# Summing the last layer's modulation on ScalarE, GpSimd and VectorE beside the second FFN, in place of TensorE beside the even mixer

## The chip, the cores and the metric

One core of a Trainium2 chip runs the whole program in one launch. The metric is the device time in microseconds (us). TensorE is called PE here, VectorE DVE, ScalarE ACT, GpSimd POOL and SyncE SP, as in the profile.

## The reference, cut to what matters

Two blocks of two layers each. The first block works on 256 tokens `x` alone (a gated delta rule layer, then a dilated attention layer, each followed by a SwiGLU FFN). The second works on the same `x` and on a second stream of 256 tokens, `ctx`: an even mixer and a mixture of experts (MoE), then an odd mixer and a MoE. Each layer modulates its normalized input with six vectors of 1024 that come from a condition vector:

```python
def second_block(...):
    sc = jax.nn.silu(c)
    sc_ctx = jax.nn.silu(c_ctx)
    for i in range(DEPTH):
        last = i == DEPTH - 1
        m = (sc @ w_ada[i] + b_ada[i]).reshape(bsz, 1, N_MOD, D_MODEL)
        mc = (sc_ctx @ w_ada[i] + b_ada[i]).reshape(N_MOD, D_MODEL)
        h_lat = modulate(rmsnorm(x, norm_mix[i]), m[:, :, 0], m[:, :, 1])
        h_ctx = modulate(rmsnorm(ctx, norm_mix[i]), mc[0], mc[1])
        ...                                   # even or odd mixer
        x = x + m[:, :, 2] * y_lat
        h_lat = modulate(rmsnorm(x, norm_ffn[i]), m[:, :, 3], m[:, :, 4])
        x = x + m[:, :, 5] * ec_moe(h_lat, ...)
        if not last:
            ...                               # the same for ctx with mc[2] to mc[5]
    return x
```

In the last layer (`i = 1`) `ctx` is not updated any more, so of `mc` only the first two vectors are used there. `w_ada[1]` is 1024 x 6144 in float32, 25 MB.

## The kernel before, in words

The stages follow one another: delta rule layer, first FFN (`ffn0`), dilated attention, second FFN (`ffn1`), even mixer (`even`), MoE 0, odd mixer (`odd`), MoE 1. A scheduler sets the order of the instructions on each engine from the order in the code and the data they wait for; after that every engine runs its own list strictly in order. Tiles of weights pass through a ring of 1 MB tiles (`rawt`, seven of them in an FFN, four in `even`), which SP loads in the order of its own list.

A dense product in float32 precision is made of three passes (`mm3`, L395 to L397): ACT rounds a weight tile to `whi` (L386), DVE or POOL subtracts to get `wlo` (L390; in `ffn1` the first four on POOL, all others on DVE; in `even` every third on POOL), and PE multiplies. One `whi`/`wlo` pair is called a split here; there are three buffers of each. `ffn` first makes the 2816 hidden columns in steps of 512 (weights `w_ffn_in`, two halves, 8 splits of 1024 elements a step and one last step of half the width), then sums 22 splits of `w_ffn_out`.

A modulation is made in three units of 2048 columns (`ada_unit`); unit 0 holds the first two of the six vectors. A unit is a generator that works through its weights in 8 pieces of 1 MB and stops after each; `fill(n)` lets the generators in the list `self.bg` do n pieces more, wherever the code has such a call: before a step of a dense product, or beside every second head of the attention. There are three ways to make a unit:

- on PE (L217): for each of 8 rows of tiles four products 128x32 by 128x512 into four groups of columns of one bank, for both streams together (`lhs2`, 16 columns each). The trace has two records for each product, so x8 in it is one piece.
- on DVE (L235, L237): the tile times one number of the condition per partition, added to an accumulator of 128x1024, and at the end products with ones (L240, two for each half of a unit) that add over the partitions.
- with `pool` (L231, L233): ACT multiplies a tile of 128x1024 into `adap`, POOL adds it to the accumulator; two such pairs a piece (the first of eight goes straight to the accumulator), and the same products with ones.

Each ends with the bias (L243) and four transposes (L247). The last layer's units are made on PE within `even`, one piece before each dense step and the others beside the heads of the attention; when they are done, `odd_shift` (L1370: 8 products of 416 columns and 8 of 160) turns the first vector of both streams into a bias for the odd mixer.

## Time and profile before

| | |
|---|---|
| median of three runs | 2474.03 us (2466.05 to 2476.62) |
| the profiled execution's own time | 2479.58 us |
| its span in the trace | 2477.8 us |
| busy share of the span: PE, DVE, ACT, POOL | 86%, 45%, 31%, 13% |
| mean DMA rate over the span | 273 GB/s |

Times within the program are counted from the start of the span. The busy shares are means over stages with different limits: in the FFNs and most of the even mixer PE has work at nearly every moment, in the two MoE stages the transfers of the experts' weights run at over 420 GB/s. The stages that matter here are the second FFN, from about 912 to 1117 us, and the even mixer, from there to about 1307 us.

### The profile page before, as it was taken

How to read it: one execution, taken by the hardware profiler on the slowest of the kernel's cores; microseconds unless marked ns; L12 is line 12 of the kernel's file. 1: busy time of each engine (PE TensorE's matmuls, PEld its weight loads, DVE VectorE, ACT ScalarE, POOL GpSimd, SP SyncE). 2: the span in 40 equal slices, each digit the busy share in tenths (PEclk: the TensorE clock that was granted, in tenths of full speed). 3: DMA queues.
4: the chain of work that ended last, by engine and by line, in shares of the span. 5: the costliest groups of instructions: out<-in, count | busy, mean ns of one | idle time of the engine just before them, and what ended most of it. 6: DMA issues, size and time to landing. Idle time of an engine off the chain costs nothing.

```text
span 2477.8 us, 30472 instructions
## 1 busy us (share of the span) xinstructions
PE 2141.7 (86%) x12141; PEld 1308.6 (53%) x12141; DVE 1107.2 (45%) x2064; ACT 777.0 (31%) x1478; POOL 316.6 (13%) x332
## 2 busy tenths in 40 slices
PE   6987988998999979998988988878888988777767
PEld 3874676786677757885577232222265662222222
DVE  3776347856555465546754121212057741101111
ACT  3564344443555444444443100000036630000000
POOL 3343211112000040003401000000021010000000
PEclk8988999999999879999998999999999989989999
DMA  9657767976332355437745999999931359999999
GB/s 351 238 173 238 231 221 223 358 259 214 118 117 83 103 190 179 161 121 263 298 169 212 403 425 426 425 425 428 420 112 62 133 243 426 423 427 425 427 426 361
DMA packets 152447, 677.58 MB, mean 273 GB/s; under 512 B 15938, under 2 KB 38316, under 8 KB 113649
## 3 DMA queue, kind: packets, MB, share of 16 engines
q1 hardware_dynamic: 143072, 637.98, 66.4%
q0 software_dynamic: 6784, 36.48, 4.3%
q8 instruction: 96, 1.57, 0.3%
q10 hardware_dynamic: 2448, 1.18, 0.2%
q14 instruction: 47, 0.38, 0.0%
HBM read 667.07 MB, written 8.52 MB: 273 GB/s over the span
## 4 chain that ended last, share of the span: by engine, by line
PE 54%; DMA 33%; DVE 8%; ACT 2%; issue 2%; POOL 1%; SPq 0%; DVEq 0%; ACTq 0%; POOLq 0%
DMA rawb<-in_w_exp_down 9%; DMA rawb<-in_w_exp_up 9%; PE mmt L395 6%; PE mmt L396 6%; PE mmt L397 6%; DMA rawt<-in_w_exp_down 5%; PE anyt L1833 4%; DMA rawt<-in_w_ada 3%; PE anyt L396 3%; PE anyt L397 3%; PE anyt L395 3%; PE anyt L1800 2%; PE adat L217 2%; DMA rawb<-in_w_exp_gate 2%; PE anyt L1816 1%
## 5 line engine op out<-in xcount | busy, mean ns | idle before, releaser
L390 DVE TENSOR_TENSOR wlo<-rawt,whi 128x1024 fp32r<-128x1024 f32 (+2 forms) x257 | 306.8, 1199 | 233.9 <-ACT whi L386 221.6
L386 ACT CAST whi<-rawt 128x1024 fp32r<-128x1024 f32 (+3 forms) x284 | 280.5, 995 | 316.0 <-PE mmt L397 118.3
L1847 PE MATMUL anyt<-rawb,xs 128*32 128x512 f32 x672 | 159.9, 637 | 54.6 <-DMA rawb<-in_w_exp_gate 28.5
L1833 PE MATMUL anyt<-rawb,xs 128*32 128x512 f32 x1472 | 170.8, 601 | 27.3 <-DMA rawb<-in_w_exp_up 15.3
L1807 DVE TENSOR_TENSOR y<-anyt,g 32x512 f32<-32x512 f32 (+1 forms) x120 | 66.4, 553 | 210.7 <-PE anyt L1800 209.2
L1800 PE MATMUL anyt<-rawb,hT 128*32 128x256 f32 (+1 forms) x1056 | 133.9, 490 | 26.3 <-DMA rawb<-in_w_exp_down 14.5
L397 PE MATMUL anyt<-whi,lo 128*128 128x512 f32 (+1 forms) x384 | 146.1, 382 | 6.4 <-DVE lo L332 6.4
L396 PE MATMUL anyt<-wlo,hi 128*128 128x512 f32 (+1 forms) x384 | 146.9, 384 | 1.4 <-DVE wlo L390 1.4
L395 PE MATMUL anyt<-whi,hi 128*128 128x512 f32 (+1 forms) x384 | 135.6, 384 | 0.0
L1852 DVE TENSOR_TENSOR h<-anyt,h 64x512 f32<-64x512 f32 x16 | 11.1, 693 | 278.3 <-ACT h L1851 278.3
L1851 ACT ACTIVATE h<-anyt 64x512 f32<-64x512 f32 x16 | 9.4, 589 | 395.7 <-PE anyt L1847 395.7
L1837 ACT ACTIVATE h<-anyt 128x512 f32<-128x512 f32 x16 | 9.6, 597 | 380.2 <-PE anyt L1833 380.2
L1847 PEld LDWEIGHTS anyt<-rawb,xs 128*32 128x32 f32 x672 | 38.5, 116 | 170.6 <-issue 95.6
L1833 PEld LDWEIGHTS anyt<-rawb,xs 128*32 128x32 f32 x1472 | 48.3, 111 | 144.7 <-issue 116.3
L1838 DVE TENSOR_TENSOR h<-anyt,h 128x512 f32<-128x512 f32 x16 | 11.1, 692 | 217.7 <-PE anyt L1833 195.0
L1800 PEld LDWEIGHTS anyt<-rawb,hT 128*32 128x32 f32 (+1 forms) x1056 | 50.0, 128 | 100.0 <-issue 65.4
L217 PE MATMUL adat<-rawt,lhs 128*32 128x512 f32 x448 | 76.7, 685 | 26.6 <-DMA rawt<-in_w_ada 22.5
L390 POOL TENSOR_TENSOR wlo<-rawt,whi 128x1024 fp32r<-128x1024 f32 (+1 forms) x27 | 67.3, 2496 | 222.5 <-ACT whi L386 216.2
L1847 PE MATMUL anyt<-rawt,xs 128*32 128x512 f32 x352 | 77.7, 596 | 10.4 <-DMA rawt<-in_w_exp_gate 7.2
L397 PEld LDWEIGHTS anyt<-whi,lo 128*128 128x128 f32 x384 | 73.2, 191 | 21.4 <-DVE lo L332 7.3
L396 PEld LDWEIGHTS anyt<-wlo,hi 128*128 128x128 f32 x384 | 73.2, 191 | 20.8 <-issue 3.2
L395 PEld LDWEIGHTS anyt<-whi,hi 128*128 128x128 f32 x384 | 72.5, 191 | 16.2 <-issue 0.8
(625 smaller groups left out, 4461.8 us busy)
## 6 DMA issues: line engine op xcount, KB each, us to landing
rawt<-in_w_ada SPq DMA_DIRECT2D x96, 1024.0 KB, 7.0
rawb<-in_w_exp_up SPq DMA_DIRECT2D x41, 2048.0 KB, 26.7
rawb<-in_w_exp_down SPq DMA_DIRECT2D x41, 2048.0 KB, 27.0
rawb<-in_w_exp_gate SPq DMA_DIRECT2D x39, 2048.0 KB, 26.6
rawt<-in_w_exp_gate SPq DMA_DIRECT2D x41, 1024.0 KB, 27.0
rawt<-in_w_ffn_in SPq DMA_DIRECT2D x40, 1024.0 KB, 7.9
rawt<-in_w_exp_up SPq DMA_DIRECT2D x38, 1024.0 KB, 27.1
rawt<-in_w_exp_down SPq DMA_DIRECT2D x31, 1024.0 KB, 26.7
```

Source lines behind the costliest of these rows:

```text
L217: nc.tensor.matmul(bank[32 * j:32 * j + 32, :], lhs[:, k, :], r[:, 0, 512 * j:512 * j + 512], start=(k == 0), stop=(k == 7))
L386: nc.scalar.copy(hi, w)
L390: e.tensor_tensor(out=lo, in0=w, in1=hi.bitcast(F32), op=OP.subtract)
L395: nc.tensor.matmul(ps, xh, wh, start=start, stop=False)
L396: nc.tensor.matmul(ps, xh, wl, start=False, stop=False)
L397: nc.tensor.matmul(ps, xl, wh, start=False, stop=stop)
L1800: nc.tensor.matmul(yb[o:o + M, c:c + n], hT[:, k, :], w[:, i * n:i * n + n], start=(k == 0), stop=(k == KT - 1), **({} if S == 2 else dict ...
L1807: nc.vector.tensor_tensor(out=ys[s][p0:p0 + CAP, 256 * q:256 * (q + n)], in0=yb[o:o + CAP, c:c + 256 * n], in1=g2[o:o + CAP, 256 * q:256 * ...
L1816: nc.tensor.matmul(ps, cols[s][:, t * P:t * P + P], rows[s][:, c:c + n], start=True, stop=True)
L1833: nc.tensor.matmul(b[CAP * i:CAP * i + CAP, :], lhs(k0 + j, i % 2), r[:, j, 512 * hf:512 * hf + 512], start=(k0 + j == 0), stop=(k0 + j == ...
L1838: nc.vector.tensor_tensor(out=h, in0=banks[1], in1=h, op=OP.mult)
L1847: nc.tensor.matmul(b[o:o + 32, :], lhs(k0 + j), r[:, j, 512 * hf:512 * hf + 512], start=(k0 + j == 0), stop=(k0 + j == KT - 1), tile_posit ...
```

## The change

`even` no longer has the three units of the last layer in its list, and only `odd_shift` is left there. `ffn1` gets four units in its list instead: unit 0 for `ctx` on DVE, then units 0, 1 and 2 for `x` with `pool`, with two `adap` buffers. Units 1 and 2 are not made for `ctx`, where nothing reads them. Since a unit now makes one stream alone, the weights of unit 0 are loaded twice: 32 pieces of 1 MB, where there were 24. `ffn1` makes four pieces before each hidden step but the first (20 in all), and one before each of the 11 tiles of `w_ffn_out`; the last follows behind the FFN.

```diff
@@ ada_unit
-    def ada_unit(self, w, b, unit, lhs, modc, two, dve=None, then=None, pool=False):
+    def ada_unit(self, w, b, unit, lhs, modc, two, dve=None, then=None, pool=False, stream=None):
...
-                        w1 = self.scv[:, k + j:k + j + 1]
+                        o = k + j + (0 if stream is None else 8 + 8 * stream)
+                        w1 = self.scv[:, o:o + 1]
                         if pool:
-                            p = acc if k + j == 0 else self.accv.tile([P, 1024], F32, name="adap", tag="adap", bufs=1)
+                            p = acc if k + j == 0 else self.accv.tile([P, 1024], F32, name="adap", tag="adap", bufs=pool)
                             nc.scalar.activation(p, r[:, j, :], AF.Copy, scale=w1)
                             if k + j:
                                 nc.gpsimd.tensor_tensor(out=acc, in0=acc, in1=p, op=OP.add)
...
@@ ffn
-                        self.scv = self.small(8)
+                        self.scv = self.small(24)
                         nc.gpsimd.tensor_copy(self.scv[:, 0:1], hi[:, 7, 255:256].bitcast(F32))
-                        nc.gpsimd.tensor_copy(self.scv, self.sc[:, 0:8])
+                        nc.gpsimd.tensor_copy(self.scv, self.sc)
                     self.fill(4)
...
             for k0 in range(0, NH, 2):
+                if key == "ffn1":
+                    self.fill()
                 raw = self.load_w(w_out[k0 * P:(k0 + 2) * P, :], 2, D)
@@ even
-            self.accp = es.enter_context(tc.tile_pool(reuse_waits="tile", name="eva", bufs=1))
-            self.bg = [self.ada2(1, u) for u in range(3)] + [self.odd_shift()]
+            self.bg = [self.odd_shift()]
@@ block1_layers
             with ExitStack() as ea:
-                if l == 0:
-                    self.accv = ea.enter_context(self.tc.tile_pool(reuse_waits="tile", name="adav", bufs=1))
+                self.accv = ea.enter_context(self.tc.tile_pool(reuse_waits="tile", name="adav", bufs=1))
+                if l:
+
+                    self.bg = [self.ada_unit(I["w_ada_2"][1], I["b_ada_2"][1], u, None, self.mod2[1], False, True, pool=2 * (st == 0), stream=st)
+                               for u, st in ((0, 1), (0, 0), (1, 0), (2, 0))]
+                else:
                     self.bg = [self.dsw_tables(self.accv)] + [ada(1, u) for u in range(3)]
```

On ACT, in the middle of the second FFN's hidden steps, the rows of before are these (`whi` are the roundings of weight tiles, `t` the SiLU of a step, `hh` the rounded hidden columns):

```order
L315 CAST hh<-tpt 128x4x128 x2
L386 CAST whi<-rawt 128x1024 x2
L476 ACTIVATE t_8183<-anyt 128x512
L386 CAST whi<-rawt 128x1024
L476 ACTIVATE t_8193<-anyt 128x512
L386 CAST whi<-rawt 128x1024 x5
```

and now, at the same place, the products `adap` and `adaacc` of the modulation (L233 here, L231 before) stand between them:

```order
L317 CAST hh<-tpt 128x4x128 x2
L388 CAST whi<-rawt 128x1024
L233 ACTIVATE adaacc<-rawt,smt 128x1024
L388 CAST whi<-rawt 128x1024
L233 ACTIVATE adap<-rawt,smt 128x1024
L478 ACTIVATE t_8635<-anyt 128x512
L233 ACTIVATE adap<-rawt,smt 128x1024
L388 CAST whi<-rawt 128x1024
L478 ACTIVATE t_8645<-anyt 128x512
L233 ACTIVATE adap<-rawt,smt 128x1024
L388 CAST whi<-rawt 128x1024
```

There is now about one such product for each rounding, from the first of them (18 of the FFN's 70 splits stand ahead of it) to the end of the FFN: 48 products, 42 of which are followed by an addition on POOL, beside 44 whole and 8 half splits; the last three stand behind the last rounding and ahead of the next norm.

On PE, between the second FFN's last product and the first products of the even mixer's projection, the rows of before are these (`xn` are the transposes of the normalized `x`, `mmt<-t` the products that spread the gate over the partitions):

```order
L217 MATMUL adat<-rawt,lhs_108 32x512 x8
L287 MATMUL mmt<-t_9139,cst 128x512
L287 MATMUL mmt<-t_9144,cst 128x512
L217 MATMUL adat<-rawt,lhs_108 32x512 x4
L310 MATMUL tpt<-cst,xn 128x128 x8
L217 MATMUL adat<-rawt,lhs_108 32x512 x4
L310 MATMUL tpt<-cst,xn 128x128 x8
```

and now these, of which L1373 is `odd_shift` (L1370 before):

```order
L312 MATMUL tpt<-cst,xn 128x128 x8
L289 MATMUL mmt<-t_9423,cst 128x512
L289 MATMUL mmt<-t_9428,cst 128x512
L242 MATMUL adat<-adaacc,cst 32x512 x2
L249 MATMUL tpt<-cst,brow 128x128 x4
L1373 MATMUL adat<-rawt 128x416 x8
L312 MATMUL tpt<-cst,xn 128x128 x4
L397 MATMUL mmt<-whi,h2i_9433 128x512
```

Four pieces of the modulation left this place; the end of the last unit (L242, L249) and the `odd_shift`, which stood in the attention, came to it.

On PE, in the first half of the even mixer's attention, the rows of before were these (`sct` are the scores, `e` the exponentials that are transposed, `acct` the products with the values):

```order
L217 MATMUL adat<-rawt,lhs_108 32x512 x3
L1347 MATMUL sct<-eK_9112,eQ 128x512
L1347 MATMUL sct<-eK_9113,eQ 128x512
L217 MATMUL adat<-rawt,lhs_108 32x512
L1347 MATMUL sct<-eK_9112,eQ 128x512
L1347 MATMUL sct<-eK_9113,eQ 128x512
L1135 MATMUL tpt<-cst,e 128x128 x4
L217 MATMUL adat<-rawt,lhs_108 32x512 x4
L1150 MATMUL acct<-va__9114,pt 128x128 x4
```

and now only the attention's own:

```order
L1350 MATMUL sct<-eK_9399,eQ 128x512
L1350 MATMUL sct<-eK_9400,eQ 128x512
L1139 MATMUL tpt<-cst,e 128x128 x4
L1350 MATMUL sct<-eK_9399,eQ 128x512
L1350 MATMUL sct<-eK_9400,eQ 128x512
L1154 MATMUL acct<-va__9401,pt 128x128 x4
```

The pieces of the modulation between the heads are gone from this list.

## Rows read from the trace of the kernel before

**Rows 1.** The page: the span, and the busy time of each engine.
```profile
span 2477.8 us, 30472 instructions
PE 2141.7 (86%) x12141; PEld 1308.6 (53%) x12141; DVE 1107.2 (45%) x2064; ACT 777.0 (31%) x1478; POOL 316.6 (13%) x332
```

**Rows 2.** Windows: us; busy PE, PEld, DVE, ACT, POOL; clock, DMA share, GB/s.
```profile
458.00:510.00 52.00, 52.00 (x235) 40.08 (x234) 42.61 (x43) 23.18 (x27) 9.12 (x5) 1.00 0.94 347
985.00:1045.00 60.00, 60.00 (x274) 48.87 (x273) 30.85 (x32) 25.68 (x31) 0.00 (x0) 1.00 0.45 148
1117.00:1137.00 20.00, 11.43 (x52) 4.06 (x51) 16.35 (x34) 12.84 (x26) 6.10 (x3) 0.83 0.93 338
1137.00:1212.00 75.00, 72.18 (x358) 49.12 (x356) 58.00 (x79) 30.18 (x54) 39.27 (x31) 0.98 0.67 240
1213.00:1258.00 45.00, 42.03 (x252) 23.79 (x244) 28.96 (x63) 22.00 (x53) 4.46 (x7) 1.00 0.78 290
1258.00:1307.00 49.00, 42.69 (x278) 37.89 (x279) 24.60 (x53) 17.21 (x43) 3.62 (x7) 0.90 0.37 137
1320.00:1730.00 410.00, 351.77 (x2364) 131.61 (x2367) 88.06 (x150) 33.60 (x56) 12.49 (x14) 0.95 0.94 397
```

**Rows 3.** The same view, of L217 alone: busy PE, PEld; clock, DMA, GB/s.
```profile
1117.00:1137.00 20.00, 6.33 (x32) 0.95 (x32) 0.83 0.93 338
1137.00:1212.00 75.00, 14.62 (x66) 2.10 (x66) 0.98 0.67 240
1213.00:1258.00 45.00, 13.87 (x94) 2.29 (x86) 1.00 0.78 290
```

**Rows 4.** The chain that ended last, in order of time: start, us, what.
```profile
484.66 0.44 PE tpt L247 x4
...
581.58 0.98 PE adat L240 x4
582.57 0.43 PE mmt L396
...
1064.66 0.94 PE mmt L395 x4
1067.46 0.93 PE mmt L395 x4
...
1134.77 1.86 PE adat L217 x8
...
1186.85 0.99 PE adat L217 x8
...
1245.91 5.59 PE adat L1370 x16
```

**Rows 5.** Timeline of POOL, then DVE, about 100 us: start, us, engine, line.
```profile
100.19 2.41 POOL L233 TENSOR_TENSOR adaacc<-adaacc,adap 128x1024 f32<-128x1024 f32 x1 [2.10 <-ACT adap L231]
...
103.99 3.17 POOL L233 TENSOR_TENSOR adaacc<-adaacc,adap 128x1024 f32<-128x1024 f32 x1
...
101.09 2.59 DVE L390 TENSOR_TENSOR wlo<-rawt,whi 128x1024 fp32r<-128x1024 f32 x1 [0.45 <-ACT whi L386]
...
103.68 1.22 DVE L390 TENSOR_TENSOR wlo<-rawt,whi 128x1024 fp32r<-128x1024 f32 x1
```

**Rows 6.** Groups by line: 925 to 1105 us, then L233's and `rawt`'s (ns min/median/max).
```profile
L390 DVE TENSOR_TENSOR wlo<-rawt,whi 128x1024 fp32r<-128x1024 f32 x56 | 68.6, 1225 | 71.2 <-ACT whi L386 71.2
L390 DVE TENSOR_TENSOR wlo<-rawt,whi 128x512 fp32r<-128x512 f32 x8 | 5.5, 691 | 5.7 <-ACT whi L386 5.7
...
L233 POOL TENSOR_TENSOR adaacc<-adaacc,adap x14: 2340/2397/3168, 100.2 to 172.8; 128x1024 f32<-128x1024 f32 x14
...
L231 ACT ACTIVATE adap<-rawt,sc x14: 1127/1144/1155, 99.0 to 171.6; 128x1024 f32<-128x1024 f32 x14
```

**Rows 7.** Timeline of ACT in the attention: first exponentials of both halves, and the last.
```profile
1220.22 0.70 ACT L1039 ACTIVATE e<-sct,smt 128x512 f32<-128x512 f32 x1
...
1258.65 0.71 ACT L1039 ACTIVATE e<-sct,smt 128x512 f32<-128x512 f32 x1
...
1281.12 0.69 ACT L1039 ACTIVATE e<-sct,smt 128x512 f32<-128x512 f32 x1 [1.29 <-PE tpt L1135]
```

More of the change, by code (lines that the diff above doesn't have):

```diff
@@ L245, in ada_unit @@
         for s in range(4):
-            src = rows[:, s::4] if two and unit else rows[:, P * s:P * s + P]
+            src = rows[:, s::4] if (two or stream is not None) and unit else rows[:, P * s:P * s + P]
             nc.tensor.transpose(tp[:, P * s:P * s + P], src, self.ident)
@@ L249, in ada_unit @@
             nc.vector.tensor_copy(
-                modc[:, st, unit * 16:unit * 16 + 16].rearrange("p (j s) -> p s j", s=4),
+                modc[:, stream or st, unit * 16:unit * 16 + 16].rearrange("p (j s) -> p s j", s=4),
                 tp.rearrange("p (s j r) -> p s j r", s=4, r=32)[:, :, :, 16 * st])
```

## The prediction

> **What bounds the kernel now.** I read the page first. PE is busy for 86% of a span of 2477.8 us [rows 1], but that is a mean over stages, so the next view was the busy time of each engine by stage [rows 2]. In the second FFN (985 to 1045) PE is busy for 60.00 of 60 us at its full clock, with DVE at 30.85, ACT at 25.68, POOL at nothing and the transfers at 0.45 of their time: PE alone sets the pace there, and what stands on the other engines has cover. Between the FFN and the even mixer (1117 to 1137) PE is busy for 11.43 of 20 us; the norm of `x` sets the end of that gap, and 6.33 us of PE's work in it are L217 [rows 3], which cost nothing there. In the even mixer's projection (1137 to 1212) PE is busy for 72.18 of 75 us, but DVE for 58.00: remove work from PE, and DVE is close behind. In the first half of the attention (1213 to 1258) PE is busy for 42.03 of 45 us, DVE only for 28.96; the second half (1258 to 1307) has no L217, and PE is busy for 42.69 of 49 us there. Behind that, MoE 0 (1320 to 1730) has the transfers at 0.94 of their time and 397 GB/s: its stream of weights starts as the mixer's memory comes free, so a shift of the mixer's end should shift all that follows by as much. So the change is worth what it takes from 1137 to 1307, less what it adds between 912 and 1137.
>
> **What it removes from PE.** L217 is busy for 14.62 us in the projection and 13.87 us in the first half of the attention [rows 3]; one piece (x8) takes 0.99 us on the chain [rows 4]. The `odd_shift`, which moves, took 5.59 us for its wider bank [rows 4], and 160/416 of that, 2.15 us, for the narrower one (an estimate): 7.7 us. Three times four transposes at 0.44 us [rows 4] go as well.
>
> **A. PE in the FFN: +9.6 us.** Half a unit ends with a pair of products with ones: 0.98 us, and the next product takes 0.43 us in place of its usual 0.23, a quarter of the 0.94 us that four take [rows 4]. Seven of the eight halves end inside the FFN: 7 x 1.18 = 8.3 us. Three of the four sets of transposes: 3 x 0.44 = 1.3 us. PE is full there, so all of it lengthens the FFN. For less there would have to be gaps in PE's row, and it shows none.
>
> **B. The additions on POOL against the subtractions on DVE: +6 us, between 0 and +18.** The rows at 100 us show what happens when both want to run: a `wlo` that starts at 101.09 during an addition (100.19 to 102.60) takes 2.59 us, where its mean in the FFN is 1.225 us [rows 6]; an addition that starts at 103.99 during a `wlo` (103.68 to 104.90) takes 3.17 us, where the median is 2.397 [rows 5, 6]. In both, what is over the usual time is what was left of the other's. They take turns. From the first product of `pool` to the FFN's end there are 42 additions, 42 x 2.40 = 101 us, and 44 whole and 8 half `wlo`, 44 x 1.225 + 8 x 0.69 = 59.4 us: 160 us, of which the last three additions, 7.2 us, follow the last split: 153 us. PE takes 2.80 us for a whole split (1064.66 to 1067.46) [rows 4]: 44 x 2.8 + 8 x 1.4 = 134.4 us, with 9.6 us of term A and about 3.5 us of its own transposes (32 at a quarter of 0.44) 147 us. Three buffers of `whi` and `wlo` let DVE be two splits late, 5.6 us, before PE feels it. So 153 us have to go into 153 us. Nothing is left over, and ACT, which holds the products (1.144 us each [rows 6]) and the roundings in one list, will not always have the next one ready. At best nothing is lost. At worst each addition delays the split behind it: 2.40 + 1.225 = 3.62 us a pair against 147/48 = 3.06 us, 42 times 0.56 is 23.7 us, less 5.6: 18 us. I take a third of that, since the first half of these instructions has the whole slack ahead of it.
>
> **C. Transfers in the FFN: +1.5 us, between 0 and +6.** A hidden step takes 4 tiles of `w_ffn_in` and 4 pieces, 8.4 MB, in 22.4 us of PE, with A and the transposes about 24.5: 342 GB/s. The first FFN did just that from 458 to 510, 347 GB/s at a share of 0.94, with PE at 52.00 of 52 us [rows 2]. At the 338 GB/s of 1117 to 1137 a step would take 24.8 us, five times 0.3 more. For 6 us a tile would have to come late at two or three places in SP's list.
>
> **D. The gap before the projection: +11 us, between +7 and +17.** Now the last pair of products with ones, its bias, four transposes and the wide half of `odd_shift` stand between the first and the second half of `xn`'s transposes, the narrow half soon after: 0.98 + 0.44 + 7.7 = 9.1 us at full clock, against one piece of L217 (1.86 us at 1134) that stood there: +7. The bias waits for DVE, and PE has been idle before: the clock of 1117 to 1137 is 0.83, and the eight records that take 0.99 us at 1186 (2.4 GHz) took 1.86 us at 1134, the 1.2 GHz level [rows 2, 4]. I add 4 us for both, and 10 us as the most, if all of `odd_shift` runs at that level and the second tile of `w_in_even`, whose place in the ring `odd_shift` holds, comes late. ACT's list puts `odd_shift`'s result ahead of the second half of the norm, so that waits with it.
>
> **E. The projection: -11 us, between -5 and -15.** PE's part without L217 is 72.18 - 14.62 = 57.6 us, DVE's 58.0 [rows 2, 3]. With both at their limit it would take 58 in place of 75 us, -17; but each waits for the other (bank, norm, rotation, transposes), and D's late start brings PE's and DVE's work closer together. I take two thirds.
>
> **F. The attention: -13 us, between -9 and -16.** The first half loses 13.87 + 7.7 + 0.9 = 22.5 of PE's 42 us. What it is then bound by, its second half shows: the 16 exponentials of the first half take 38.4 us (1220.22 to 1258.65), those of the second 23.2 us (to 1281.81) [rows 7]. The difference, 15.2 us, is about the most that can go. Since the first half's late products run beside the second half's exponentials, and the stretch between cannot shrink under DVE's 28.96 us (45 - 29 = 16), I take 13.
>
> **The sum.** 9.6 + 6 + 1.5 + 11 - 11 - 13 = +4.1 us. Against the profiled execution's own time, 2479.58 + 4.1 = 2483.7 us; that execution is 0.22% over the median, so 2483.7 x 2474.03 / 2479.58 = **2478 us** in terms of the median. 0.5% of it, 12.4 us, is about what a measurement of this kernel can tell from no change.
>
> **The rivals.**
> *The additions and the subtractions decide: slower.* B at its worst, 18 us, with the rest as above, gives 9.6 + 18 + 1.5 + 11 - 11 - 13 = +16 us: 2490 us. For it speaks that 153 us of turns have 153 us of room; against it, that POOL and DVE had idle time before in the same stretch [rows 2], and that ACT, which waits for a free `adap`, keeps POOL's backlog at two. It decides from B = 14 us on. The Trainium skill, SBUF — State Buffer, "Who interferes with whom", states the rule behind it: a VectorE instruction with two SBUF inputs and a GpSimd instruction that reads SBUF hold a shared read interface for the whole instruction, and the second one to come blocks until the first is done. By that rule no part of the 101 us may overlap with the 59 us; the trace agrees, with 2.59 us where 1.225 is usual and 3.17 where 2.40 is. No sum above needs the rule.
> *The even mixer gives back all that it can: faster.* B and C at nothing, D at 8, E at -15, F at -16: 9.6 + 8 - 15 - 16 = -13.4 us, 2461 us. For it speaks that PE is busy for 57 of 60 parts of the stretch from 1137 to 1258; against it, DVE's 58 us in the projection, and that the second half of the attention, without any L217, still takes 49 us.
> *The second FFN becomes bound by its transfers:* C at 6 us, +8.6 us in all, 2483 us, still within no change. For it speaks that the first FFN runs at 0.94 of the transfers' time; against it, that PE there has no gap.
>
> **How the numbers follow.** I give the forecast, the sum within 12.4 us of nothing (the transfers' case in it), 0.46; the first rival, with other mishaps of its sign (D at its worst gives the same), 0.31; the second 0.23. All terms at their low ends make -14 us, at their high ends +37 us; the range leaves out the far part of the latter: from -15 to +21 us, 2459 to 2495 us. The forecast's own range is 2466 to 2490 us. So faster 0.23, same 0.46, slower 0.31.
>
> **What the profile of the changed kernel would show.** A: in the second FFN pairs of products with ones at 0.98 us. B: `wlo` with a mean well over 1.225 us, POOL's additions well over 2.40, and PE waiting for `wlo` or `whi` between 980 and 1120; if PE has no gap there, B is nothing. C: PE waiting for `rawt`. D: the first projection product 25 to 36 us behind the FFN's last one (20 us before). E: DVE busy for over 90% of the projection. F: the first half's exponentials within 23 to 29 us. I would be wrong upwards if PE's gaps in the FFN add up to over 14 us, and downwards if the projection ends within 85 us of the FFN's last product (95 us before) and F holds as well.

## The result, and the profile after

The changed kernel takes 2494.64 us (median of 4 runs, 2488.29 to 2496.57), the kernel before on the same chip 2470.52 us (4 runs, 2466.05 to 2476.62): a ratio of 1.0084, 95% interval 1.0057 to 1.0112. It is slower. The forecast was 2478 us and no change; the time lies inside its range (2459 to 2495 us), 0.4 us below the upper end. The profiled executions are 14.0 us apart (spans 2477.8 and 2491.8): that of before was 9 us above the median of its runs here, so the stages below add up to 14 us and not to 24. There is one trace of each kernel, and the stages are compared by it.

The page's head answers to [rows 1]: PE's total hardly moved, DVE has 79 us more, POOL 121 us more.

```profile
span 2491.8 us, 30365 instructions
...
PE 2136.3 (86%) x11985; PEld 1312.9 (53%) x11985; DVE 1186.4 (48%) x2079; ACT 827.0 (33%) x1526; POOL 437.4 (18%) x375
```

The windows by stage, with the columns of [rows 2]: the second FFN, the gap behind it, the projection, the two parts of the attention, MoE 0. L218, the products that [rows 3] show as L217, no longer stands in the even mixer.

```profile
990.00:1060.00 70.00, 67.91 (x331) 52.90 (x330) 61.08 (x40) 49.41 (x58) 55.40 (x22) 1.00 0.83 297
1131.00:1163.00 32.00, 13.93 (x43) 6.84 (x41) 24.34 (x33) 10.97 (x21) 17.29 (x11) 0.68 0.26 93
1163.00:1230.00 67.00, 60.45 (x295) 50.42 (x293) 50.64 (x73) 35.03 (x62) 34.15 (x26) 0.95 0.56 185
1230.00:1264.00 34.00, 23.37 (x121) 17.82 (x122) 27.77 (x52) 18.71 (x47) 5.12 (x4) 0.80 0.12 40
1264.00:1297.00 33.00, 27.22 (x159) 23.44 (x158) 21.19 (x46) 15.43 (x39) 0.60 (x1) 0.79 0.09 29
1335.00:1745.00 410.00, 355.10 (x2362) 132.15 (x2365) 88.31 (x151) 33.60 (x56) 12.48 (x14) 0.95 0.94 397
```

The gap is 32 us where it was 20, with PE busy for 13.93 us at a clock of 0.68. The projection is shorter and no engine in it is full: PE 60.45, DVE 50.64 of 67 us. In the first part of the attention PE is idle for a third of the time and in the second for a sixth, at a clock of 0.80 and 0.79. MoE 0 is what it was.

Inside the second FFN, the groups that answer to [rows 6] (953 to 1122 us; the subtractions, the additions, the products of ScalarE):

```profile
L392 DVE TENSOR_TENSOR wlo<-rawt,whi 128x1024 fp32r<-128x1024 f32 (+1 forms) x57 | 121.9, 2163 | 23.3 <-ACT whi L388 23.3
...
L235 POOL TENSOR_TENSOR adaacc<-adaacc,adap 128x1024 f32<-128x1024 f32 x38 | 113.2, 2979 | 73.1 <-ACT adaacc L233 69.0 <-ACT adap L233 2.2
...
L233 ACT ACTIVATE adap<-rawt,smt 128x1024 f32<-128x1024 f32 x39 | 44.8, 1152 | 23.4 <-POOL adaacc L235 21.2 <-DMA kd<-cxka 2.2
```

A subtraction takes 2.16 us, an addition 2.98, as the taking of turns in [rows 5] announced. But PE hardly shows it: these are all its waits from 940 us to the FFN's end (us in total, times, longest), and under them the products with ones in it (ns min/median/max). The ends of PE's records are modelled: records of 0.40 us start 0.23 us apart, so a delay of less than the difference does not show as a wait. The comparison of marks below finds 7 us.

```profile
PE anyt L398 <- DVE wlo L392: 1.6, 3, 0.7
PE mmt L398 <- DVE wlo L392: 1.0, 4, 0.3
PE adat L242 <- POOL adaacc L235: 0.5, 1, 0.5
```

```profile
L242 PE MATMUL adat<-adaacc,cst x28: 592/605/617, 954.5 to 1114.2; 128*32 128x512 f32 x28
```

The gap, engine by engine (timeline: start, us, engine, line). POOL's backlog first:

```profile
1136.31 2.79 POOL L235 TENSOR_TENSOR adaacc<-adaacc,adap 128x1024 f32<-128x1024 f32 x1
1139.05 2.54 POOL L1367 COPY rawt<-mod 128x1024 f32<-128x1024 f32 x2
1141.56 2.03 POOL L285 TENSOR_TENSOR t<-cst,mod 128x512 f32<-128x512 f32 x2
1143.55 2.33 POOL L235 TENSOR_TENSOR adaacc<-adaacc,adap 128x1024 f32<-128x1024 f32 x1
```

The FFN's last product started at 1130.90. POOL comes to the copies for `odd_shift` (L1367), to the diagonals with which the gate is spread (L285) and to the last addition only 8, 10 and 12 us after 1131.30, where it ended. PE's list in the same stretch, and under it the norm's transposes of the kernel before, whose FFN ended at 1117.86:

```profile
1147.03 1.08 PE L312 MATMUL tpt<-cst,xn 128*128 128x128 f32 x4 [15.73 <-DVE smt L159]
1149.66 1.09 PE L312 MATMUL tpt<-cst,xn 128*128 128x128 f32 x4 [1.55 <-DVE t L330]
1150.54 3.62 PE L289 MATMUL mmt<-t,cst 128*128 128x512 f32 x4
1154.10 1.51 PE L242 MATMUL adat<-adaacc,cst 128*32 128x512 f32 x4
1156.40 0.75 PE L249 MATMUL tpt<-cst,brow 128*128 128x128 f32 x4 [0.80 <-DVE brow L245]
1156.99 5.75 PE L1373 MATMUL adat<-rawt 128*128 128x416 f32 x16
1162.58 0.60 PE L312 MATMUL tpt<-cst,xn 128*128 128x128 f32 x4
1162.93 0.48 PE L397 MATMUL mmt<-whi,h2i 128*128 128x512 f32 x1
```

```profile
1132.98 1.79 PE L310 MATMUL tpt<-cst,xn 128*128 128x128 f32 x8 [2.67 <-DVE smt L159]
...
1136.57 1.09 PE L310 MATMUL tpt<-cst,xn 128*128 128x128 f32 x8
```

PE stands still for 15.73 us, waiting for the norm, and only then does what could have filled that wait: the gate (L289), the last unit's products and transposes (L242, L249) and the wide half of `odd_shift` (L1373), 12.0 us from 1150.54 to 1162.58. The first transposes of the norm come 15.7 us behind the end of the FFN's last product, against 15.1 before; the ninth record of them, 18.7 before, comes at 31.3. The norm is hardly late; what stands between its halves is. The last unit's products need the last addition, which ended at 1145.88, 1.2 us ahead of the norm's transposes: they could not have filled the wait in any order. `odd_shift` could have begun in it, as its copies ended at 1141.59, but in PE's list it stands behind the last unit.

The chain of the projection's start shows the other half of the price:

```profile
1165.95 1.10 PE adat L1373 x8
1167.07 5.47 DMA rawt<-in_w_in_even
1172.56 1.05 ACT whi L388
1173.64 1.24 DVE wlo L392
1174.92 0.50 PE mmt L398
```

The first four of the eight products of `odd_shift`'s narrow half end at 1167.05, and with them the first of its two tiles of weights comes free; a tile of `w_in_even` starts at 1167.07. PE goes on with the projection's next split at 1173.66, after 2.29 us of waiting for its `whi`, and with its `wlo` at 1174.92.

Last, the exponentials that answer to [rows 7] (the first, the seventeenth and the last of 32):

```profile
1245.32 0.69 ACT L1043 ACTIVATE e<-sct,smt 128x512 f32<-128x512 f32 x1
...
1263.05 0.68 ACT L1043 ACTIVATE e<-sct,smt 128x512 f32<-128x512 f32 x1
...
1295.82 0.69 ACT L1043 ACTIVATE e<-sct,smt 128x512 f32<-128x512 f32 x1 [1.28 <-PE tpt L1139]
```

### The profile page after: what moved, and what is told of

The parts are those of the page before. It is cut to its first block, busy times and chain, and to the rows that moved or that the text cites. A ratio compares the mean times of both kernels' runs of the same rounds, so it can differ in the third digit from the quotient of the medians.

```text
span 2491.8 us, 30365 instructions
## 1 busy us (share of the span) xinstructions
PE 2136.3 (86%) x11985; PEld 1312.9 (53%) x11985; DVE 1186.4 (48%) x2079; ACT 827.0 (33%) x1526; POOL 437.4 (18%) x375
## 3 DMA queue, kind: packets, MB, share of 16 engines
q10 hardware_dynamic: 2448, 1.18, 0.2%
## 4 chain that ended last, share of the span: by engine, by line
PE 49%; DMA 32%; DVE 11%; ACT 3%; issue 2%; POOL 2%; SPq 0%; DVEq 0%; ACTq 0%; POOLq 0%
DMA rawb<-in_w_exp_up 10%; DMA rawt<-in_w_exp_up 9%; DMA rawb<-in_w_exp_down 6%; PE mmt L398 5%; PE mmt L397 5%; PE mmt L399 5%; PE anyt L1836 4%; DMA rawt<-in_w_ada 3%; DVE wlo L392 3%; PE anyt L1803 3%; PE anyt L398 3%; PE anyt L399 3%; PE anyt L397 2%; PE anyt L1819 1%; PE anyt L1690 1%
## 5 line engine op out<-in xcount | busy, mean ns | idle before, releaser
L392 DVE TENSOR_TENSOR wlo<-rawt,whi 128x1024 fp32r<-128x1024 f32 (+2 forms) x257 | 363.7, 1426 | 182.4 <-ACT whi L388 172.2
L1836 PE MATMUL anyt<-rawb,xs 128*32 128x512 f32 x1472 | 172.4, 607 | 24.5 <-DMA rawb<-in_w_exp_up 13.4
L235 POOL TENSOR_TENSOR adaacc<-adaacc,adap 128x1024 f32<-128x1024 f32 x56 | 159.0, 2840 | 102.6 <-ACT adaacc L233 74.7
L1803 PE MATMUL anyt<-rawb,hT 128*32 128x256 f32 (+1 forms) x1056 | 143.2, 526 | 27.3 <-DMA rawb<-in_w_exp_down 15.6
L1427 POOL TENSOR_TENSOR owl<-rawt,owh 128x832 fp32r<-128x832 f32 x4 | 7.7, 1956 | 425.3 <-ACT owh L1426 425.3
```

The costliest lines, as they stand in the source:

```text
L235: nc.gpsimd.tensor_tensor(out=acc, in0=acc, in1=p, op=OP.add)
L392: e.tensor_tensor(out=lo, in0=w, in1=hi.bitcast(F32), op=OP.subtract)
L1803: nc.tensor.matmul(yb[o:o + M, c:c + n], hT[:, k, :], w[:, i * n:i * n + n], start=(k == 0), stop=(k == KT - 1), **({} if S == 2 else dict ...
L1836: nc.tensor.matmul(b[CAP * i:CAP * i + CAP, :], lhs(k0 + j, i % 2), r[:, j, 512 * hf:512 * hf + 512], start=(k0 + j == 0), stop=(k0 + j == ...
```

## The experiments

Each was timed against the kernel before on the same chip (its medians there 2471.7 to 2473.8 us; two chips in all, so that the ratios compare best). From each trace I took five marks: the first transposes of a hidden step of the second FFN, the FFN's last product, the first reduction of a projection bank on DVE (L1015 of before), the first exponential, and the attention's last product. At the first mark the first unit's additions on DVE have begun, but none of its products with ones has come on PE (the first pair has in e5, e9 and f_hold2). Behind the mark stand 723 of the FFN's own products where no unit is finished in the FFN, 730 in e9 and f_hold2, and 720 in the others; at 0.23 us each, the FFN's column is good to 1 us, and about 2 us too long in those two. What lies outside the marks takes 2118 to 2133 us in the fourteen traces; that the edits have no part in this is not shown.

```
us                     median  ratio to before, 95%    FFN   gap  bank chain  att.  odd_shift
before                 2470.5  -                     162.6  19.6  34.0  68.4  85.0 127.9
after                  2494.6  1.0084 1.0057-1.0112  177.8  31.6  50.5  63.5  74.7  25.7
e1_shift_late          2477.9  1.0028 1.0010-1.0046  177.8  20.2  37.5  64.1  75.0  81.6
e2_removed_only        2459.1  0.9960 0.9944-0.9975  162.6  19.4  32.1  64.4  73.5  76.7
e3_added_only          2494.6  1.0105 1.0085-1.0125  177.8  24.2  44.3  66.7  78.3 138.1
e4_no_additions        2467.5  0.9984 0.9970-0.9998  174.4  17.3  28.6  64.0  71.0   4.5
e5_all_dve             2468.2  0.9975 0.9960-0.9991  171.1  18.9  30.3  63.9  73.8   5.9
e6_removed_shift_early 2457.3  0.9932 0.9912-0.9951  162.6  18.8  29.9  63.1  72.1   4.5
e7_last_dve            2480.0  1.0022 1.0007-1.0037  177.4  20.2  32.4  64.3  75.5   4.5
e8_three_dve           2470.4  0.9981 0.9965-0.9998  172.6  18.9  30.9  64.2  75.8   4.5
e9_earlier             2513.6  1.0159 1.0137-1.0180  206.8  24.3  42.9  63.2  72.7  16.1
f_hold4                2481.0  1.0033 1.0018-1.0048  169.4  24.6  41.5  64.0  71.1  18.2
f_hold2                2468.2  0.9987 0.9973-1.0000  169.8  20.4  36.7  63.8  74.2  14.0
g_hold4_late           2473.6  1.0010 0.9992-1.0029  170.4  23.5  38.5  64.5  73.3  82.8
```

FFN: first mark to the FFN's last product. Gap: from there to the first product of the projection. Bank: from the FFN's last product to the first reduction. Chain: from there to the first exponential. Att.: to the attention's last product. Odd_shift: where its first product starts, in us behind the FFN's last product. The first exponential stands at bank plus chain; so in e1, e2 and g_hold4_late `odd_shift`, whose code stands in the attention, ran before that, in the chain (76.7 us against 96.5 in e2), and only in the kernel before and e3 in the attention.

**e1_shift_late.** `odd_shift` out of the projection:

```diff
-            self.bg = [self.odd_shift()]
             ew = ExitStack()
...
             ew.close()
+            self.bg = [self.odd_shift()]
```

> The change, with odd_shift kept out of the projection and run in the attention, as the kernel before had it. Theory (the even mixer, freed of the three units, is held by VectorE's chain of norms and rotations; odd_shift in front of the projection is a price on top of that): the gap between the FFN's last and the projection's first product falls from 31.6 us to about 25, the wait for w_in_even's second tile goes, the attention hides odd_shift's 7.7 us, and 5 to 8 us of the change's 24 are given back: about 2488 us. Rival 1 (odd_shift's place alone ate the gain of the mixer that was forecast): 13 us or more back, at most 2481 us. Rival 2 (the gap is set by the norm and by the last unit's second half): 2 us or less, 2493 us.

It gives back 14 us by the ratios and 17 by the medians, 13.0 of it before the first reduction (50.5 to 37.5): rival 1. `odd_shift`'s 7.7 us are hidden, though not in the attention: it runs at the end of the chain, which takes 64.1 us against 63.5. Rival 2 falls.

**e2_removed_only.** The kernel before, without the units and `eva`:

```diff
-            self.accp = es.enter_context(tc.tile_pool(reuse_waits="tile", name="eva", bufs=1))
-            self.bg = [self.ada2(1, u) for u in range(3)] + [self.odd_shift()]
+            nc.gpsimd.tensor_copy(self.mod2[1], self.mod2[0])
...
             ew.close()
+            self.bg = [self.odd_shift()]
```

> The kernel before without the three units in the even mixer and with nothing put in their place; the last layer's modulation is left out (the layer before's is copied there), odd_shift stays in the attention. It measures what their removal is worth, without any price in the second FFN or in the gap. Theory (the mixer is held by VectorE once TensorE is freed, so about 11 us come out of it, as the trace of the changed kernel has it): 2470.5 - 11 = 2459 us, with VectorE busy for over 85% of the projection. Rival 1 (24 us, as was forecast, are there, and odd_shift's new place ate them): 2446 us. Rival 2 (nothing of it was on the path): 2470 us.

2459.1 us, as the theory had it: removal alone is worth 10 us by the ratio and 13 by the medians, not 24. Yet the theory's reason is not quite right: the columns bank and chain lose 1.9 and 4.0 us, the attention 11.5, and neither PE nor DVE is full in the chain (below). The columns add up to 17.4 us, more than the times give; the profiled execution of the kernel before took 9 us more than its median, so what its stages give for the removal may be a few us too much. And `odd_shift` moved too: some of the attention's 11.5 us are those that `odd_shift` took there, about 7.7 of PE's, and it now runs in the chain.

**e3_added_only.** The change, with the three units and `odd_shift` of the kernel before kept in `even`:

```diff
-            self.bg = [self.odd_shift()]
+            self.accp = es.enter_context(tc.tile_pool(reuse_waits="tile", name="eva", bufs=1))
+            self.bg = [self.ada2(1, u) for u in range(3)] + [self.odd_shift()]
```

> The change, and the kernel before's three units in the even mixer as well: everything is paid and nothing removed. Theory (8 us of TensorE's inserted products and transposes and 8 us of waits for late splits in the second FFN, and a gap a few us longer for the last unit's second half): 2470.5 + 16 + 3 = 2490 us. Rival (the FFN costs only TensorE's inserted work, and the rest of the change's loss is odd_shift's place in the gap): 2479 us.

22 us over the kernel before of those runs by the medians, 26 by the ratio: the FFN pays 15.2 us as in the change, the bank comes 10.3 us later than before. The rival falls; the theory's 3 us for the gap were too few.

**e4_no_additions.**

```diff
-                            if k + j:
+                            if k + j and stream is None:
                                 nc.gpsimd.tensor_tensor(out=acc, in0=acc, in1=p, op=OP.add)
```

> The change without GpSimd's additions in the second FFN: ScalarE's products, the loads, VectorE's unit and TensorE's inserted work stay, the sums of three units are left out (so the last layer's modulation is wrong in values). Theory (the additions and VectorE's subtractions take turns, and 7.6 us of waits in the FFN are theirs): the mean of wlo in the second FFN falls from 2.05 us to about 1.25, TensorE's waits there go, 2487 us. Rival 1 (the waits come from ScalarE's list, in which 48 products stand between the roundings): 2493 us. Rival 2 (the additions cost the gap as well, through the last unit's backlog on POOL): 2483 us or less.

Rival 2, and by far: 25 us (ratios) to 27 us (medians) less than the change. The mean subtraction falls to 1153 ns; of the gain the FFN gives only 3.4 (4.7, if one counts that the last unit's products now stand inside it); 21.9 us lie between the FFN's end and the first reduction, where `odd_shift` now starts at 4.5 us instead of 25.7. Without the additions the FFN is still 2.6 us longer than its inserted work (174.4 - 162.6 - 9.2).

**e6_removed_shift_early.** e2, with `self.bg = [self.odd_shift()]` ahead of the projection.

> As the run with the three units removed from the mixer and nothing added (the last layer's modulation is left out, the layer before's copied), but with odd_shift in front of the projection, where the change puts it. Theory (odd_shift's products there cost nothing as long as GpSimd has no backlog: they fill a gap in which TensorE waits for the norm, and the projection then starts at 2.4 GHz): gap about 18 us, projection about 60 us (69 with odd_shift late), total 5 to 11 us below that run: 2448 to 2454 us. Rival (odd_shift's 7.7 us and the tile that its loads hold up cost their time there, and the change lost 11 us to them): 2467 us.

Gap and projection are as the theory said (18.8 and 58.6 us), the ratio is 0.28% below that of e2, the median 1.8 us; the forecast of 2448 to 2454 us was missed by 3 us. `odd_shift` at this place costs nothing: the bank comes 2.2 us sooner than in e2. So its place in the program is not the price; the price is what it has to wait behind. These windows (columns of [rows 2]) show the gap of e2, where PE is idle for two thirds of the time at a clock of 0.62, and its projection:

```profile
1110.60:1130.00 19.40, 6.82 (x21) 3.87 (x21) 15.70 (x32) 12.77 (x26) 5.87 (x3) 0.62 0.45 149
1130.00:1199.00 69.00, 63.70 (x297) 51.52 (x296) 57.77 (x80) 32.17 (x56) 41.59 (x32) 0.96 0.33 109
```

The 10 us between the two projections (69.0 and 58.6) are not what the theory made of them. The 201st of the 240 products starts 50.6 us behind the first in e2 and 48.5 in e6; the rest comes behind it, where the wide half of `odd_shift` now stands among e2's last products for 5.3 us.

**e5_all_dve, e7_last_dve, e8_three_dve.** The units' engine, one by one (`0` is DVE, `2` ScalarE and POOL; the change is 0, 2, 2, 2; e7 has 0, 2, 2, 0 and e8 0, 2, 0, 0):

```diff
-    ..., self.mod2[1], False, True, pool=2 * (st == 0), stream=st)
-        for u, st in ((0, 1), (0, 0), (1, 0), (2, 0))]
+    ..., self.mod2[1], False, True, pool=p, stream=st)
+        for u, st, p in ((0, 1, 0), (0, 0, 0), (1, 0, 0), (2, 0, 0))]
```

> The change with all four units summed on VectorE (product and addition in one instruction of 1.28 us), none on GpSimd and ScalarE; odd_shift in front of the projection as in the change. Theory (the additions' backlog on GpSimd, behind the FFN's end, makes the norm late, TensorE stands still and the projection starts at half clock; without it odd_shift fits into the gap): the gap falls from 31.6 to about 18 us, the projection to about 60 us, the FFN takes 2 to 4 us more for VectorE's bursts: about 2469 us. Rival (VectorE, with 61 us more to do in the FFN, makes TensorE wait there): FFN 10 us or more longer, 2480 us or more.

> The change with the last unit alone moved from ScalarE and GpSimd to VectorE: units one and four on VectorE, two and three on GpSimd. Theory (what costs is the backlog behind the FFN's end, not the turns inside it): gap 18 us, projection 60 us, FFN as in the change or 2 us longer: about 2472 us. Rival (the turns inside the FFN cost as much, since GpSimd still adds 28 times there): 2485 us.

> The change with the last two units moved to VectorE: only the second unit is added on GpSimd. Theory (as for the run with the last unit moved): 2470 us, since the gap is free of GpSimd in both. Rival (each unit on VectorE costs TensorE its own waits in the FFN): 3 us or more above the run with one unit moved.

e5 hits: 2468.2 us, faster than the kernel before (ratio 0.9975, interval 0.9960 to 0.9991) and 26 us faster than the change. One part of the forecast missed: the FFN was to be 2 to 4 us longer and is 6.7 us shorter than the change's. Its gap, in the timeline of PE:

```profile
1123.02 1.05 PE L242 MATMUL adat<-adaacc,cst 128*32 128x512 f32 x4
1125.47 0.75 PE L249 MATMUL tpt<-cst,brow 128*128 128x128 f32 x4 [1.39 <-DVE brow L245]
1128.99 7.52 PE L1373 MATMUL adat<-rawt 128*128 128x416 f32 x16 [2.78 <-DMA rawt<-in_w_in_odd]
1136.35 1.88 PE L289 MATMUL mmt<-t,cst 128*128 128x512 f32 x4
...
1138.67 1.09 PE L312 MATMUL tpt<-cst,xn 128*128 128x128 f32 x8
```

The same last unit, wide half of `odd_shift` and gate as in the change now stand ahead of the norm's transposes, which come 15.6 us behind the FFN as there. On DVE the units are nearly free, in the FFN too. The group of the subtractions in it (953 to 1122 us), and the windows of the gap and the projection:

```profile
L392 DVE TENSOR_TENSOR wlo<-rawt,whi 128x1024 fp32r<-128x1024 f32 (+1 forms) x58 | 66.5, 1148 | 14.3 <-ACT whi L388 14.3
```

```profile
1123.10:1142.00 18.90, 14.73 (x59) 8.98 (x60) 14.60 (x33) 12.31 (x26) 5.73 (x3) 0.91 0.56 170
1142.00:1201.70 59.70, 55.58 (x276) 46.73 (x274) 50.26 (x71) 31.99 (x55) 35.73 (x26) 0.97 0.58 196
```

e8 hits in its time (2470.4 us). e7 (2480.0) lies between theory and rival: the last unit's backlog is gone from the gap (bank 32.4), but its FFN costs as much as the change's. Up the row of e5, e8, e7 (none, one, two units on POOL) the FFN takes 171.1, 172.6 and 177.4 us.

**e9_earlier.**

```diff
-                    self.fill(4)
+                    self.fill(5 if key == 'ffn1' else 4)
```

> The change, with five pieces instead of four pulled into each hidden step of the second FFN: the same three units are added on GpSimd, but the last addition comes before the FFN's end and not 15 us behind it. Theory (of the change's loss some 20 us come from the additions that run on behind the FFN's end: the last unit's products, its bias, and odd_shift, which uses the same bank, stand on TensorE behind the last addition, and the second half of the norm and the projection behind these; the turns inside the FFN are worth only about 7): gap 19 us, projection 60 us, FFN as in the change or 1 to 3 us longer: 2477 us. Rival (turns on the port are the price, wherever they fall; more of them now fall on the FFN): 2487 us or more.

The rival was right, in its number (2487 us or more) and, inside the FFN, in its mechanism; the theory was wrong. The FFN takes 29 us more than the change's (27, counted from the same product): from the second one on, a hidden step with five pieces takes 31 to 33 us instead of 23 to 25. In the middle of such a step a subtraction takes twice its 1.15 us, the next starts 3.3 us behind it, where PE needs 2.80 for a split [rows 4], and POOL adds without a pause:

```profile
1011.75 2.26 DVE L392 TENSOR_TENSOR wlo<-rawt,whi 128x1024 fp32r<-128x1024 f32 x1 [1.06 <-ACT whi L388]
1015.08 2.28 DVE L392 TENSOR_TENSOR wlo<-rawt,whi 128x1024 fp32r<-128x1024 f32 x1 [1.07 <-ACT whi L388]
```

```profile
1003.93 22.40 POOL L235 TENSOR_TENSOR adaacc<-adaacc,adap 128x1024 f32<-128x1024 f32 x7 [4.45 <-ACT adaacc L233]
```

Laid over each other, the two kinds cover 29.4 of this step's 30.9 us. In the change they cover the same step's 24.5 us wholly, with 7 additions in place of 9: there the turns just fit beside PE. ACT's waits for a free `adap` (29.1 us, 25.0 in the change) are how the turns reach the roundings behind them in its list. Why the stretch of `w_out` is 9.5 us longer as well, with fewer additions, stays open.

And although the last addition now ends 24.8 us ahead of the FFN's end, `odd_shift` still stands behind the norm's first transposes (at 16.1 us), and the bank comes at 42.9 us. Here its weights were late: SP issued the load of their second tile 8.7 us behind the FFN's end, and it took 5.0 us to land. So what costs is that this work runs behind the norm's first transposes; a late POOL is one way to get it there, and not the only one.

**f_hold4, f_hold2, g_hold4_late.** All units on DVE, with the products, bias and transposes of four (or of the last two) held back until the FFN's end by a tile of ones that is written after the first add of the output:

```diff
+        one = self.accv.tile([P, 32], F32, name="one", bufs=1)
+        nc.gpsimd.tensor_scalar(out=one, in0=self.x[:, 0, 0:32], scalar1=0.0, scalar2=1.0, op0=OP.mult, op1=OP.add)
+        for s in sums:
+            self.ada_end(modc, *s, one)
```

> All four units on VectorE, and their products with ones, biases and transposes held back until the FFN's end (their four sums wait in eight buffers; the ring of weights in the FFN has three tiles less for it). Theory (TensorE's inserted work costs its full 8 us inside the FFN, which has no gap, and less in the gap behind it, where TensorE waits for the norm): from the first hidden step to the FFN's end 163 us as without any unit (171 with them inside), the gap 3 to 6 us longer than the 18.9 of the run with all units on VectorE: 2464 us against 2468. Rival 1 (the four units' chains of product, bias, transpose and copy, at half clock, take the 8 us back in the gap): 2468 to 2475 us. Rival 2 (the smaller ring makes TensorE wait for weights): the FFN at 168 us or more.

> As the run before, but the first unit (both parts of it, which odd_shift needs) is finished inside the FFN and only the last two are held back; the ring has one tile less. Theory: 4 us of inserted work stay in the FFN (167 us), odd_shift can start in the gap without waiting for them: gap 19 to 21 us, 2465 us. Rival (what is held back costs its time in the gap): 2468 us or more.

> All four units on VectorE and held back as above, and odd_shift in the attention, as in the kernel before. Theory (the held products take the place of odd_shift as what fills the gap and keeps TensorE from its half clock, and 7.7 us less stand in front of the second half of the norm): gap 20 us, 2 to 3 us below the run with odd_shift early, 2462 us. Rival (odd_shift is cheaper in the gap than in the attention): above it by 2 us or more.

All three missed their times. The FFN takes 169 to 170 us (168 in f_hold2, counted from the mark of before) instead of 163 and 167; in f_hold4 the smaller ring makes ACT wait 28.6 us for weights. The held products do fill the wait for the norm, but they push `odd_shift` behind its first transposes, to 14 or 18 us, and in g_hold4_late the norm's transposes themselves to 19.2: banks at 36.7 to 41.5 us. f_hold2's gap (20.4 us) is as its theory said, its time as its rival said. Rival 2 of f_hold4 is seen, and rival 1 in its mechanism, with 2481 us above its 2468 to 2475. g_hold4_late is 7 us faster than f_hold4, where 2 to 3 were expected, so its rival falls.

## Where the prediction was right and where it was wrong, step by step

The time is inside the range, by 0.4 us; the sign was given too little chance, and the forecast of no change was wrong. That it is inside is luck: the terms D and E erred the same way by 5.5 and 6.1 us, F by 2.7, and only the width given to the range held them.

**A, PE in the FFN: +9.6; measured 8.0.** The 28 records of products with ones take 6.9 us from start to start, the twelve transposes 1.1. Right, with the price on the next product overestimated (0.98 us a pair, not 1.18).

**B and C: +6 and +1.5; measured 7.2 together.** The FFN is 15.2 us longer (177.8 against 162.6), 8.0 of it A. PE waited for no tile of weights, so C is nothing and B 7.2. Not all of it is turns: without additions 2.6 us remain (e4), with all units on DVE 1.1 (171.1 - 162.6 - 7.4, of which e5's first pair stands ahead of the mark); whether ACT's products make the difference is not shown. B was right inside the FFN, and so was its arithmetic, 153 us of turns into 153 us. But it had three additions, 7.2 us, follow the last split, and gave them no cost: POOL's last addition ended 14.6 us behind the FFN's last product, and the last unit, with `odd_shift` behind it, had to wait for it. The Trainium skill, SBUF — State Buffer, "Who interferes with whom", says that of a VectorE instruction with two SBUF inputs and a GpSimd instruction that reads SBUF the later one blocks until the other is done; the trace agrees, with 2163 ns for a subtraction beside the additions and 1153 in e4, where the additions are left out.

**D, the gap: +11, between +7 and +17; measured +12.0 to the first product, +16.5 to the first finished bank.** The order on PE was the one that the prediction describes, and the late tile of `w_in_even`, which it put at the far end of D, came (1167.07 to 1172.56). What failed is the step that took these for fixed costs of `odd_shift` and of the last unit. e4 to e8 have `odd_shift` in the same gap, e5, e7 and e8 the end of the last unit as well, and their bank comes at 28.6 to 32.4 us, sooner than before (34.0). The price is that this work stood behind the norm's first transposes instead of in the 15 us in which PE waits for them.

How much each has: without additions and with `odd_shift` late the bank comes at 32.1 us (e2); additions alone make it 37.5 (e1), `odd_shift` early alone 29.9 (e6), both together 50.5. So 5.4 us are the additions' and the last unit's, -2.2 `odd_shift`'s, and the other 15.2 us of the 18.4 arise only when both meet. e4 has both but the additions themselves, and its bank comes at 28.6 us: it is the additions, and not the last unit's work on PE.

**E, the projection: -11; measured -4.9 from the first bank to the first exponential.** I took two thirds of a gain in which PE or DVE would be full. Neither is. This is the window of the change from the first reduction to the first exponential:

```profile
1181.80:1245.30 63.50, 50.53 (x251) 41.93 (x249) 53.93 (x75) 28.73 (x50) 36.81 (x29) 0.91 0.45 149
```

DVE is busy for 85% and PE for 80% of it. The stretch takes 63.1 to 64.5 us in all twelve kernels that have no unit of PE's in the mixer, whatever came before, and 68.4 and 66.7 in the two that have (before, e3): it is a chain of norms, rotations and transposes handed between DVE, POOL and PE, and PE's 14.6 us of L217 [rows 3] were mostly in its gaps: without them the stretch got 4 to 5 us shorter. That it is such a chain is read from the trace; no run shortened a link of it. The sign that I named, DVE over 90%, did not come.

**F, the attention: -13; measured -10.3.** The mechanism was right, as far as `odd_shift` and the units left PE there and the first half took most of the gain. The split was misread: by 1258.65 us of [rows 7] 19 of the 32 exponentials had begun, not 16. From the first to the seventeenth it took 26.0 us before (to 1246.19) and 17.7 after, so the 38.4 us of the prediction and its sign of 23 to 29 us rest on the misreading. All 32 took 61.6 us before and 51.2 after.

**The sum.** 15.2 + 16.5 - 4.9 - 10.3 = +16.5 us, and -2.4 for what lies outside the marks: the 14 us between the profiled executions. Of the 12.4 us between this and +4.1 the bank has 5.5, E 6.1 and F 2.7, less 1.9 that the FFN cost less. The first rival named what decided (the additions: without them e4 is 0.16% under the kernel before), but put it into the FFN, where it cost 7 us, and not behind it.

**Open:** whether POOL's lateness made the scheduler put `odd_shift` behind the norm's first transposes in the change, or another rule of its order (e9 has that order without late additions); and what the last 3 to 4 us in the FFN of f_hold4 and g_hold4_late are, where no unit's products stand in it and PE's waits there make 3.5 and 3.8 us of the 6.8 and 7.8.

## What to carry to other kernels

Work that was added to the gap between two stages was free here (8 to 9 us of it, in a wait of 15) where it stood in the list ahead of what the gap waits for, and made the next stage's first bank 20 us later in the change, where it stood behind (50.5 us against 30.3 in e5); look in the order for what stands behind that wait, and ask which of its operands come from the engine with the backlog. Where VectorE and GpSimd both read two operands from SBUF, each addition on GpSimd took by my estimate 1.5 us from VectorE (57 subtractions longer by 1.0 us, beside 38 additions): with VectorE half idle, one instruction there that multiplies and adds (1.30 us in e5) was cheaper than a product on ScalarE and an addition on GpSimd (2.98 us), by 26 us in all, most of it through the order in the gap. And removing PE's work from a stage is worth only what its chain of other engines leaves: here 10 to 13 us of 28.5.

## What the runs showed of the hardware

- A short instruction on VectorE with operands in SBUF can wait out an addition on GpSimd as a long one does: a 128x1 `smt` of the norm, 0.16 us elsewhere, took 2.26 us from 1143.64 on, until the addition of 1143.55 to 1145.88 had ended.

```profile
1143.64 2.26 DVE L160 SCALAR_TENSOR_TENSOR smt<-smt 128x1 f32<-128x1 f32 x1
...
1146.98 0.16 DVE L160 SCALAR_TENSOR_TENSOR smt<-smt 128x1 f32<-128x1 f32 x1
```

- TensorE's granted clock fell in the gap of the change, in which it did nothing for 15.7 us, to 0.60 and stayed low behind it (0.55), at or near the 1.2 GHz level, while the gate, the last unit and the norm's transposes ran; in e5, where the same work is spread over the gap, it was 0.91. The gate's four records took 3.62 us in the change and 1.88 in e5.

```profile
1131.30:1147.00 15.70, 0.00 (x1) 0.00 (x1) 14.76 (x20) 4.59 (x13) 14.58 (x10) 0.60 0.46 166
1147.00:1156.00 9.00, 7.03 (x16) 2.83 (x16) 2.73 (x8) 2.87 (x4) 0.00 (x0) 0.55 0.00 0
```

- Yet the cold start of the projection cost little: in its first 10 us e2 (clock 0.87, behind a gap in which PE was mostly idle) got through 41 records and e6 (1.00, behind a gap with `odd_shift` in it) through 47, and the projection's twenty-first product came 5.8 us behind the first in e2 and 4.6 in e6.

```profile
1130.00:1140.00 10.00, 10.00 (x41) 8.22 (x40) 4.30 (x9) 5.32 (x10) 1.91 (x1) 0.87 0.00 0
```

```profile
1133.70:1143.70 10.00, 10.00 (x47) 8.31 (x46) 6.98 (x11) 6.80 (x11) 2.41 (x1) 1.00 0.89 323
```
